# Inputs laid out in DRAM as they are read: weights by panel, cached keys by head dimension, values and states by head; new rows leave as they lie

## The chip, the cores and the metric

The kernel runs on one core of one Trainium2 chip. The metric is the device time of one execution in microseconds (us), the median of the runs. Arrays are laid out on the host before the launch, and what the host does with them is no part of the time. The engines are named as in the profile: PE (TensorE) with PEld for its weight loads, DVE (VectorE), ACT (ScalarE), POOL (GpSimd), SP (SyncE). DMAs are issued by SP, ACT and POOL, each on a queue of its own.

## The reference

One inference step of a layer with two groups of heads, for 1024 frames of one new stream (the prompt) and 16 frames of each of 8 running streams (the sample, 128 rows), in float32:

```
h = rms_norm(x) * norm_pre                      # x: 2048 wide
q_sb,k_sb,v_sb,gate_sb,q_r,k_r,v_r,gate_r = split(h @ w_in, 8)   # 8 x 1024, 8 heads of 128 each
A: z = q_sb k_sb^T / sqrt(128)                  # strictly causal; the sample also sees 1024 cached keys
   a = sigmoid(z) * cumprod_from_the_right(sigmoid(-z)),  o = a v_sb
B: rotary on q_r, k_r; retention in chunks of 64 with decay per head, state S (128 x 128);
   the sample starts from state_ret
y = concat(head_norm(o) * silu(gate)) @ w_out;  x + rms_norm(y) * norm_post
```

Returned are the new x of prompt and sample, the new keys and values of both, and the new states of both.

## The kernel before, in words

All weights, and the activations that meet them, are split into a high and a low part (float32r: `split`, L135, an ACT copy and a DVE subtraction), and each product is made of three matmuls. The rows are worked in two groups: group 0 holds the prompt tiles 0 to 3 and the sample, group 1 the tiles 4 to 7. For each group a loop runs over 8 heads (called 1 to 8 here), and each head makes its panels: `project` (L234, one column panel of 128 from `load_w`, 16 k-tiles of 128 rows in four loads of 256 KB) and, for two heads at once, `project_rows` (L293, values, eight loads of 256 KB). The loaded chunk is `wr` (or `wrn`), its parts `wh` and `wl`; four buffers each.

What the heads do beside their projections runs as jobs: Python generators that yield the number of ticks after which they go on. Each step of a projection calls `tick`, which lets one job make one step. This, with a scheduler that may put an instruction ahead of others that would wait, fixes the order of instructions on each engine; at run time each engine takes its own in that order. The numbers of ticks are the table `D_*`.

The jobs that matter here:

- `sb_branch` with `stick_breaking`, per head: scores `z` of a tile (L593), sigmoids `kp` and `be` on ACT (L505, L506), a select on POOL (L511), a scan and a product on DVE (L522, L523), then a turn of the weights through DRAM: `turn_out` writes `s_be`, `turn_in` reads it back in four loads (L486), a DVE transpose (L583) finishes it. The tile's output is `pa` (L623).
- `decode`, per head in group 0: the sample's scores against the cached keys, in two sets (`zc`, L672), and against its own keys (`zn`, L714); then the same weights, turned through `s_bd`; then the sum over the cached values in two sets of matmuls (`pd`, L741). Keys `kcT` and values `vc` share six buffers (tag `kv`).
- `ret_branch` and `retention`: `rk` is turned through `s_rk`, the decay table `dT` is loaded by SP, scores `rs` (L768) are multiplied by it (`sc`, L770), and `pa` (L786) follows.
- `keys_out`: transposes the new keys `kT` into rows (`kn`) and stores them 32 columns at a time.

A chunk of cached keys is loaded so:

```
for i in range(4):
    nc.gpsimd.dma_start(
        kc[32 * i : 32 * i + 32, :].rearrange("p (k d) -> p k d", d=32),
        cache_k[0, 2 * c + j, s * 512 : (s + 1) * 512, h, 32 * i : 32 * i + 32].rearrange("(k p) d -> p k d", p=32),
    )
...
turned = nc.vector.transpose(ready[-1][:, m % 2, :], loaded.pop(0))
```

DVE's transpose works in squares of 32 by 32, so the four loads place the squares and the transpose turns each. After the last head, `out_panel` and `out_project` multiply by `w_out` (L1066 to L1068), and the results are normed and stored.

Of the kernel before, what the change touches and what calls it, by code (L numbers as in the profile page):

```python
# [16 lines left out]
P = 128  # L17
D = 2048
# [13 lines left out]
D_REST = 8  # L32
KC_AHEAD = 2
D_DEC = 2
D_NAT = (8, 11)
# [3 lines left out]
D_AV = (9, 11)  # L39
D_ZC = 12  # L40
D_ROW = 18
D_KN = 40
D_VC = (6, 46)
# [22 lines left out]
def tile_hybrid_step(  # L66
# [7 lines left out]
    norm_pre,  # L74
    w_in,
    sb_gain,
# [188 lines left out]

    col = lambda i, h: i * H * P + h * P

    def project_rows(g, mov, col, dst, off, loads=None):
# [5 lines left out]
        for w in range(KT // 2):  # L274
            wr = wp.tile([P, 2, 2 * P], F32, name="wrn", tag="wr")
            nc.sync.dma_start(
                wr,
                w_in[0, 2 * w * P : 2 * (w + 1) * P, col : col + 2 * P].rearrange("(k p) e -> p k e", p=P),
            )
            for _ in range(WQ if loads and w == 0 else 0):  # L280
# [26 lines left out]
    with ExitStack() as s1:  # L307
# [152 lines left out]
        def store_rows(tiles, n, off, dst_p, dst_s, h):  # L460
            nc.scalar.dma_start(
                dst_p[0, 0, tiles[0] * P : (tiles[0] + 4) * P, h, :].rearrange("(t p) d -> p t d", p=P),
                n[:, off : off + 4, :],
            )
            if SAMPLE in tiles:
                nc.scalar.dma_start(
                    dst_s[0].rearrange("b t h d -> (b t) h d")[:, h, :], n[:, off + 4, :]
                )

# [166 lines left out]
        def decode(h, qs, rest):  # L636
# [9 lines left out]

            def chunk(m):
                s, r = divmod(m, NB)
                j, c = divmod(r, 4)
                return s, j, c  # L650

            def load(m):
                s, j, c = chunk(m)
                kc = ip.tile([P, 512], F32, name="kc", tag="kc", bufs=3)
                for i in range(4):
                    nc.gpsimd.dma_start(  # L656
                        kc[32 * i : 32 * i + 32, :].rearrange("p (k d) -> p k d", d=32),
                        cache_k[0, 2 * c + j, s * 512 : (s + 1) * 512, h, 32 * i : 32 * i + 32].rearrange(
                            "(k p) d -> p k d", p=32
                        ),  # L660
                    )
                return kc

            loaded, ready = [], []
            for m in range(-KC_AHEAD, 2 * NB + 1):
                if m > 0 and m % NB == 0:
                    s, _, _ = chunk(m - NB)
                    z = score_tile("zc")
                    for j in range(2):
                        for c in range(4):  # L670
# [3 lines left out]
                                qp[:, j, r],  # L674
                                ready[2 * j + c // 2][:, c % 2, :],
                                start=(j == 0),
                                stop=(j == 1),
                            )
                            if j == c == 0:

                                tc.add_manual_dep(
                                    mm.ins,
                                    turned.ins.name,
                                    mybir.DependencyInfo(
                                        mybir.DependencyClass.NoSync, mybir.DependencyReason.SCHED_ONLY
                                    ),
                                    reason="a set at a time",
                                )
                    ready = []
                    with tc.issue_after(mm.ins):  # L690
                        with_scores()
                    sigmoids(kp, be, s * 512, z)
                if 0 <= m < 2 * NB:
                    if m % 2 == 0:
                        ready.append(ip.tile([P, 2, 512], F32, name="kcT", tag="kv", bufs=V_BUFS))
                    turned = nc.vector.transpose(ready[-1][:, m % 2, :], loaded.pop(0))  # L696
                    yield D_ZC
                if m + KC_AHEAD < 2 * NB:
                    loaded.append(load(m + KC_AHEAD))
            def load_v(k):  # L700
                vc = ip.tile([P, NB, P], F32, name="vc", tag="kv", bufs=V_BUFS)
                ld = nc.sync.dma_start(
                    vc, cache_v[0, :, k * P : (k + 1) * P, h, :].rearrange("b p d -> p b d")
                )
                if 2 <= k < V_BUFS:
                    tied(ld)
                return vc
# [108 lines left out]
        def sample_retention(h, out, sc, rq, rkn, rv):  # L816
# [57 lines left out]
            for c in range(4):  # L874
                nc.scalar.dma_start(s_sample[0, 2 * c : 2 * c + 2, h].rearrange("b d e -> d b e"), sts[c])

# [20 lines left out]
        def sb_branch(gi, g, h, out, q2, k2, kT, rest):  # L897
            tiles, nt = g["tiles"], len(g["tiles"])
            off = 0 if gi == 0 else 4
            def keys_out():  # L900
                kn = ep.tile([P, nt * P], F32, name="kn", tag="rkn")
                nc.vector.transpose(kn, kT[:, : nt * P])
                for i in range(4):
                    q, ds = slice(32 * i, 32 * i + 32), slice(32 * i, 32 * i + 32)
                    nc.scalar.dma_start(
                        k_prompt[0, 0, tiles[0] * P : (tiles[0] + 4) * P, h, ds].rearrange("(j b) a -> b j a", b=32),
                        kn[q, : 4 * P].rearrange("p (j a) -> p j a", a=32),
                    )
                    if SAMPLE in tiles:
                        nc.scalar.dma_start(  # L910
                            k_sample[0].rearrange("b t h d -> (b t) h d")[:, h, ds].rearrange("(j b) a -> b j a", b=32),
                            kn[q, 4 * P :].rearrange("p (j a) -> p j a", a=32),
                        )
                yield 1

            Job(keys_out(), D_KN)
            if gi == 0:
# [279 lines left out]

_INS = [
    "x_prompt", "x_sample", "cache_sb_k", "cache_sb_v", "state_ret", "norm_pre", "w_in",
    "sb_head_norm", "ret_head_norm", "w_out", "norm_post",  # L1200
]
_OUTS = [
    (1, PT * P, D), (NB, DS, D), (1, 1, PT * P, H, P), (1, 1, PT * P, H, P), (1, 1, H, P, P),
    (1, NB, DS, H, P), (1, NB, DS, H, P), (1, NB, H, P, P),
]


# [60 lines left out]
```

## Time and profile before

| | |
|---|---|
| median of 3 runs | 2397.44 us (2394.52 to 2399.0) |
| profiled execution | 2393.5 us, its span 2391.8 us |
| mean granted TensorE clock | 0.991 |
| PE, DVE, ACT, POOL busy | 97%, 52%, 38%, 27% of the span |
| read from HBM, written | 336.24 MB, 79.69 MB |
| DMA packets | 677049, of them 224752 under 512 bytes |

How to read the page: its first part gives the busy time of each engine, its second the span in 40 slices (the digits are tenths), the groups give line, engine, operation, tiles out<-in, count, busy time and mean, and the idle time just before with what ended it. In a row of waits stand the waiting engine with its tile and line, what ended the wait, the sum in us, how often, and the longest. Group 0 runs from the start to about 1120 us, group 1 to about 1960 us, then the output projection.

### The profile page before, as it was taken

To read this page: it belongs to the slowest core of one execution; us is meant where nothing else is said; L and a number is where in the kernel's file an instruction comes from. 1 tells how busy PE (TensorE), PEld (TensorE's weight loads), DVE (VectorE), ACT (ScalarE), POOL (GpSimd) and SP (SyncE) were. 2 spreads that over 40 slices of the span, in tenths; PEclk is the share of its full clock that TensorE was granted. 3 is DMA by queue.
4 is the path that set the end of the run, shared out by engine and by line. 5 is a ranking of instruction groups with operands and counts; after the bars stand their busy time and mean duration, and the time that the engine had idled before them with its cause. 6 is when DMAs were issued, how large, how long until landed. Compare 5 with 4: busy or idle time off the path is not lost.

```text
span 2391.8 us, 40520 instructions
## 1 busy us (share of the span) xinstructions
PE 2320.5 (97%) x14832; PEld 2092.4 (87%) x14832; DVE 1255.6 (52%) x2442; ACT 920.0 (38%) x1937; POOL 644.1 (27%) x1033
## 2 busy tenths in 40 slices
PE   7999999999999999999899999999999999999998
PEld 7998899998999999998778989889898888888887
DVE  7245545455545555456545554554554566564544
ACT  6323333333333333334333334333343444443443
POOL 3144354434445353434202112020220220000000
PEclk9999999999999999999999999999999999999999
DMA  7659779796989979698866565555655666765563
GB/s 245 163 131 215 161 162 200 163 200 153 199 177 200 188 163 205 158 207 221 187 182 154 139 149 154 139 145 151 150 154 134 161 160 197 229 211 182 188 192 131
DMA packets 677049, 418.68 MB, mean 175 GB/s; under 512 B 224752, under 2 KB 620016, under 8 KB 674544
## 3 DMA queue, kind: packets, MB, share of 16 engines
q1 hardware_dynamic: 524272, 285.99, 48.0%
q0 software_dynamic: 32256, 71.36, 13.9%
q10 hardware_dynamic: 120320, 58.74, 9.1%
q8 instruction: 116, 1.90, 0.4%
q14 instruction: 85, 0.70, 0.1%
HBM read 336.24 MB, written 79.69 MB: 174 GB/s over the span
## 4 chain that ended last, share of the span: by engine, by line
PE 71%; DMA 6%; DVE 4%; issue 2%; ACT 2%; SPq 1%; POOL 0%; DVEq 0%; ACTq 0%; POOLq 0%
PE acc L234 36%; PE accn L293 12%; PE a L1067 5%; PE a L1066 5%; PE a L1068 5%; PE pa L623 2%; PE z L593 2%; DMA wr<-w_in 2%; PE zc L672 1%; PE pd L741 1%; DMA mr<-s_y 1%; DMA mr<-s_h 1%; DMA dT<-c_dt 1%; DVE wl L137 1%; PE pa L786 1%
## 5 line engine op out<-in xcount | busy, mean ns | idle before, releaser
L234 PE MATMUL acc<-mh,wh 128*128 128x256 f32 (+2 forms) x2304 | 667.2, 341 | 7.8 <-ACT wh L136 7.2
L137 DVE TENSOR_TENSOR wl<-wr,wh 128x512 fp32r<-128x512 f32 (+1 forms) x576 | 391.4, 684 | 517.7 <-ACT wh L136 500.8
L234 PE MATMUL acc<-ml,wh 128*128 128x256 f32 (+2 forms) x2304 | 661.5, 339 | 0.0
L234 PE MATMUL acc<-mh,wl 128*128 128x256 f32 (+2 forms) x2304 | 660.8, 339 | 0.0
L136 ACT ACTIVATE wh<-wr 128x512 fp32r<-128x512 f32 (+1 forms) x576 | 358.0, 625 | 726.6 <-PE acc L234 229.7
L234 PEld LDWEIGHTS acc<-mh,wh 128*128 128x128 f32 x2304 | 421.2, 189 | 40.5 <-ACT wh L136 9.0
L234 PEld LDWEIGHTS acc<-mh,wl 128*128 128x128 f32 x2304 | 424.5, 189 | 31.7 <-issue 2.5
L234 PEld LDWEIGHTS acc<-ml,wh 128*128 128x128 f32 x2304 | 425.5, 189 | 28.6 <-issue 0.8
L656 POOL DMA_DIRECT2D kc<-cache_sb_k x512 | 332.5, 655 | 344.4 <-DVE kcT L696 209.5
L293 PE MATMUL accn<-whn,mh 128*128 128x256 f32 x1152 | 329.2, 287 | 4.6 <-DVE rg L320 4.5
L293 PE MATMUL accn<-wln,mh 128*128 128x256 f32 x1152 | 326.3, 284 | 2.4 <-DVE wln L137 2.4
L293 PE MATMUL accn<-whn,ml 128*128 128x256 f32 x1152 | 325.9, 284 | 0.0
L293 PEld LDWEIGHTS accn<-whn,mh 128*128 128x128 f32 x1152 | 220.9, 192 | 8.5 <-DVE rg L320 4.8
L293 PEld LDWEIGHTS accn<-wln,mh 128*128 128x128 f32 x1152 | 221.7, 192 | 3.4 <-DVE wln L137 2.6
L293 PEld LDWEIGHTS accn<-whn,ml 128*128 128x128 f32 x1152 | 221.3, 192 | 0.0
L1067 PE MATMUL a<-wl,mh 128*128 128x512 f32 (+1 forms) x576 | 219.4, 381 | 1.1 <-DVE wl L137 1.1
L1066 PE MATMUL a<-wh,mh 128*128 128x512 f32 (+1 forms) x576 | 218.9, 381 | 0.1
L1068 PE MATMUL a<-wh,ml 128*128 128x512 f32 (+1 forms) x576 | 218.9, 380 | 0.0
L137 DVE TENSOR_TENSOR wln<-wrn,whn 128x512 fp32r<-128x512 f32 x128 | 87.3, 689 | 125.1 <-ACT whn L136 124.8
L136 ACT ACTIVATE whn<-wrn 128x512 fp32r<-128x512 f32 x128 | 79.6, 632 | 164.7 <-PE acc L234 70.7
L486 POOL DMA_DIRECT2D be<-s_be x128 | 94.3, 743 | 132.4 <-DMA s_be<-be 114.5
L1067 PEld LDWEIGHTS a<-wl,mh 128*128 128x128 f32 x576 | 108.3, 188 | 22.4 <-DVE wl L137 2.2
(195 smaller groups left out, 2617.6 us busy)
## 6 DMA issues: line engine op xcount, KB each, us to landing
wr<-w_in SPq DMA_DIRECT2D x384, 256.0 KB, 4.2
wr<-w_out SPq DMA_DIRECT2D x184, 256.0 KB, 3.6
wrn<-w_in SPq DMA_DIRECT2D x128, 256.0 KB, 3.3
kc<-cache_sb_k POOLq DMA_DIRECT2D x512, 64.0 KB, 4.7
vc<-cache_sb_v SPq DMA_DIRECT2D x64, 512.0 KB, 9.0
xt<-x_prompt SPq DMA_DIRECT2D x8, 1024.0 KB, 6.0
xr<-x_prompt SPq DMA_DIRECT2D x8, 1024.0 KB, 6.2
out<-out ACTq DMA_DIRECT2D x24, 256.0 KB, 3.4
```

The lines of the kernel that those rows point to most:

```text
L136: nc.scalar.activation(hi, src, AF.Copy)
L137: nc.vector.tensor_tensor(lo, src, hi.bitcast(F32), ALU.subtract)
L234: last = nc.tensor.matmul(a[:, :m], lhs[:, j, :], rhs[w][:, j, o : o + m], start=(w == 0 and j == 0 and n == 0), stop=(w == KT // WQ - 1 a ...
L293: anchor[0] = nc.tensor.matmul(a, lhs[q][:, jj, ts], rhs[:, j, :], start=(w == 0 and j == 0 and n == 0 and t % 2 == 0), stop=(w == KT // 2 ...
L486: q.dma_start(raw[32 * i : 32 * i + 32, :].rearrange("p (k a) -> p k a", a=32), s[:, :, 32 * i : 32 * i + 32].rearrange("k (j b) a -> b (k ...
L593: nc.tensor.matmul(z[:, :c], q2[a][:, i * P : (i + 1) * P], k2[b][:, s : s + c], start=(m == 0), stop=(m == 2),)
L623: nc.tensor.matmul(po[:, :P], at[:, j, :], vn[:, j, :], start=(j == 0), stop=(j == t))
L656: nc.gpsimd.dma_start(kc[32 * i : 32 * i + 32, :].rearrange("p (k d) -> p k d", d=32), cache_k[0, 2 * c + j, s * 512 : (s + 1) * 512, h, 3 ...
L672: mm = nc.tensor.matmul(z[r, :], qp[:, j, r], ready[2 * j + c // 2][:, c % 2, :], start=(j == 0), stop=(j == 1),)
L1066: nc.tensor.matmul(a[:, :width], hi[q][:, j, ts], wh, start=(k == 0), stop=False)
L1067: nc.tensor.matmul(a[:, :width], hi[q][:, j, ts], wl, start=False, stop=False)
L1068: nc.tensor.matmul(a[:, :width], lo[q][:, j, ts], wh, start=False, stop=(k == KT - 1))
```

## The change

The arrays get other layouts in DRAM, and the loads and stores follow them:

- `w_in` becomes two arrays: `w_cols` for the six column panels of each head, so that the 2 KB which a partition reads in one load lie together (before, four pieces of 512 bytes), and `w_rows` for the value panels (before, two pieces of 1 KB).
- `cache_k` has the head dimension on the partitions. A load of 512 KB brings two chunks as they are needed, 4 KB in one piece for each partition, right into the buffer of `kcT`. The tile `kc`, its 512 loads and the 128 transposes are gone. `decode` has 8 steps of 24 ticks for this where it had 16 of 12.
- `cache_v` and `state_ret` are laid out by head: a value load has 4 KB in one piece for each partition (before 8 pieces of 512 bytes), a state load 1 KB (before two of 512 bytes).
- New keys leave as `kT` lies, head dimension first, from ACT right after `kT` is made; the job `keys_out` with its transpose is gone. New values and states leave by head. The host puts them in the asked order.

```diff
+COLS = (0, 1, 3, 4, 5, 7)
+ROWS = (2, 6)
-D_ZC = 12
+D_ZC = 24
-D_KN = 40
...
@@ load_w, project_rows
-            nc.sync.dma_start(
-                wr,
-                w_in[0, w * WQ * P : (w + 1) * WQ * P, col : col + P].rearrange("(k p) e -> p k e", p=P),
-            )
+            nc.sync.dma_start(wr, w_cols[COLS.index(col[0]), col[1], :, w * WQ : (w + 1) * WQ, :])
...
-                w_in[0, 2 * w * P : 2 * (w + 1) * P, col : col + 2 * P].rearrange("(k p) e -> p k e", p=P),
+            nc.sync.dma_start(wr, w_rows[ROWS.index(col[0]), col[1] // 2, :, 2 * w : 2 * (w + 1), :])
...
@@ store_rows
-                dst_p[0, 0, tiles[0] * P : (tiles[0] + 4) * P, h, :].rearrange("(t p) d -> p t d", p=P),
-                n[:, off : off + 4, :],
+            nc.scalar.dma_start(dst_p[h, :, tiles[0] : tiles[0] + 4, :], n[:, off : off + 4, :])
...
@@ decode
-            loaded, ready = [], []
-            for m in range(-KC_AHEAD, 2 * NB + 1):
-                if m > 0 and m % NB == 0:
-                    s, _, _ = chunk(m - NB)
+            def load_k(m):
+                kc = ip.tile([P, 2, 512], F32, name="kcT", tag="kv", bufs=V_BUFS)
+                ready.append((kc, nc.gpsimd.dma_start(kc, cache_k[h, m // 4, m % 4])))
+
+            ready = []
+            for m in range(KC_AHEAD):
+                load_k(m)
+            for m in range(NB + 1):
+                if m > 0 and m % 4 == 0:
+                    s, ks = m // 4 - 1, ready[:4]
+                    del ready[:4]
...
-                                ready[2 * j + c // 2][:, c % 2, :],
+                                ks[2 * j + c // 2][0][:, c % 2, :],
...
-                if 0 <= m < 2 * NB:
-                    if m % 2 == 0:
-                        ready.append(ip.tile([P, 2, 512], F32, name="kcT", tag="kv", bufs=V_BUFS))
-                    turned = nc.vector.transpose(ready[-1][:, m % 2, :], loaded.pop(0))
+                if m + KC_AHEAD < NB:
+                    load_k(m + KC_AHEAD)
+                if m < NB:
                     yield D_ZC
-                if m + KC_AHEAD < 2 * NB:
-                    loaded.append(load(m + KC_AHEAD))
...
-                    vc, cache_v[0, :, k * P : (k + 1) * P, h, :].rearrange("b p d -> p b d")
+                ld = nc.sync.dma_start(vc, cache_v[h, k])
...
@@ sample_retention
-                tied(nc.sync.dma_start(st, state_ret[0, 2 * c : 2 * c + 2, h].rearrange("b d e -> d b e")))
+                tied(nc.sync.dma_start(st, state_ret[h, :, 2 * c : 2 * c + 2, :]))
...
@@ sb_branch
-            def keys_out():
-                kn = ep.tile([P, nt * P], F32, name="kn", tag="rkn")
-                nc.vector.transpose(kn, kT[:, : nt * P])
-                for i in range(4):
...
-            Job(keys_out(), D_KN)
+            nc.scalar.dma_start(k_prompt[h, :, tiles[0] * P : (tiles[0] + 4) * P], kT[:, :NB_TOK])
+            if SAMPLE in tiles:
+                nc.scalar.dma_start(k_sample[h], kT[:, 4 * P : 5 * P])
```

The numbers of lines are other ones after the change: the key loads L656 become L640, the selects L511 become L502, the turns L479 and L486 become L470 and L477, the weight loads L220 become L222, the value loads L702 become L680. The program has as many matmuls as before.

The order of instructions moves at two places that the prediction speaks of. The first is POOL's in the first head of group 0, before the change, from the store of the third tile's weights (`s_be_2`) to the read-back of the fourth's:

```order
L479 DMA s_be_2_2348<-kb 128x3x128
L511 AFFINE_SELECT kb<-kb 128x128 x2
L656 DMA kc<-cache_sb_k 32x16x32 x2
L486 DMA kb<-s_be_2_2348 32x12x32 x2
L511 AFFINE_SELECT kp<-kp 128x128
L511 AFFINE_SELECT be<-be 128x128
L517 AFFINE_SELECT kp<-kp 128x128
L517 AFFINE_SELECT be<-be 128x128
L486 DMA kb<-s_be_2_2348 32x12x32 x2
L479 DMA s_be_3_2513<-kb 128x4x128
L656 DMA kc<-cache_sb_k 32x16x32 x2
L486 DMA kb<-s_be_3_2513 32x16x32 x4
```

The same place on POOL after the change, with the key loads that follow for the second head:

```order
L470 DMA s_be_2_2255<-kb 128x3x128
L477 DMA kb<-s_be_1_2121 32x8x32 x4
L502 AFFINE_SELECT kb<-kb 128x128 x2
L470 DMA s_be_3_2440<-kb 128x4x128
L502 AFFINE_SELECT kp<-kp 128x128
L502 AFFINE_SELECT be<-be 128x128
L508 AFFINE_SELECT kp<-kp 128x128
L508 AFFINE_SELECT be<-be 128x128
L477 DMA kb<-s_be_2_2255 32x12x32 x4
L477 DMA kb<-s_be_3_2440 32x16x32 x4
L640 DMA kcT<-cache_k 128x1024 x6
```

The selects of `kp` and `be` are the sample's and need the sigmoids of `zn`. Before, they stood between the second and the third of the four read-backs of `s_be_2`; now all eight read-backs stand behind them. Between the read-backs and the next head stood single key loads; now six whole ones stand together.

The second place is SP's queue in the first head and the start of the second, before the change, from the first value loads (`vc`) to the decay table (`dT`) of the second head:

```order
L702 DMA vc<-cache_sb_v 128x8x128 x2
L220 DMA wr<-w_in 128x4x128 x4
L702 DMA vc<-cache_sb_v 128x8x128 x3
L220 DMA wr<-w_in 128x4x128 x2
L702 DMA vc<-cache_sb_v 128x8x128
L220 DMA wr<-w_in 128x4x128
L486 DMA be<-s_bd_2487 32x36x32 x4
L486 DMA ro<-s_rk_1_2720 32x20x32 x2
L702 DMA vc<-cache_sb_v 128x8x128 x2
L486 DMA ro<-s_rk_1_2720 32x20x32 x2
L486 DMA so<-s_o_0_4_0_2800 32x16x32 x4
L763 DMA dT<-c_dt 128x256
```

The same queue after the change (the first two value loads stand further ahead):

```order
L680 DMA vc<-cache_v 128x1024
L222 DMA wr<-w_cols 128x512 x3
L680 DMA vc<-cache_v 128x1024
L222 DMA wr<-w_cols 128x512
L477 DMA be<-s_bd_2391 32x36x32 x4
L680 DMA vc<-cache_v 128x1024 x2
L222 DMA wr<-w_cols 128x512 x2
L680 DMA vc<-cache_v 128x1024 x2
L222 DMA wr<-w_cols 128x512 x2
L477 DMA ro<-s_rk_1_2624 32x20x32 x4
L477 DMA so<-s_o_0_4_0_2706 32x16x32 x4
L739 DMA dT<-c_dt 128x256
```

The last two value loads stood in the middle of the read-backs of `rk`; now they stand four weight loads ahead of them. On PE the two sets of value matmuls of this head stood 20 projection matmuls apart and now stand 74 apart, and `zn` stands some 90 projection matmuls earlier.

More of the change, by code (lines that the diff above doesn't have):

```diff
@@ L74, in tile_hybrid_step @@
     norm_pre,
-    w_in,
+    w_cols,
+    w_rows,
     sb_gain,
@@ L1256 @@
     data = {n: np.ascontiguousarray(inputs[n]) for n in _INS}
+    data.update(_laid_out({n: np.asarray(a) for n, a in inputs.items()}))
     data.update(_constants())
@@ L1266 @@
     r = run_bass_kernel_spmd(nc, [data], core_ids=[0])
-    return tuple(r.results[0][f"out_{i}"] for i in range(len(_OUTS)))
+    got = [np.asarray(r.results[0][f"out_{i}"]) for i in range(len(_OUTS))]
+    return tuple(np.ascontiguousarray(a) for a in _as_asked(*got))
```

81 lines of the change are left out of this document (35 added, 46 removed).

## The prediction

> **What bounds the kernel now.** The page comes first: its busy times, then the rows by slice.
>
> ```profile
> span 2391.8 us, 40520 instructions
> PE 2320.5 (97%) x14832; PEld 2092.4 (87%) x14832; DVE 1255.6 (52%) x2442; ACT 920.0 (38%) x1937; POOL 644.1 (27%) x1033
> DMA  7659779796989979698866565555655666765563
> ```
>
> TensorE is busy for 97% of the span; VectorE, which loses work here, for 52%. The change leaves every matmul as it is, so what can be won is the time in which TensorE waits, and the time in which its clock is lowered after a wait. The DMA engines are close to full in the slices 5 to 20 (group 0) and have room later. Next I read the waits of TensorE alone: the sum of the waits in us, their number, the longest.
>
> ```profile
> PE p0t L379 <- DVE dg L396: 10.7, 1, 10.7
> PE pa L786 <- DVE sc L770: 8.2, 6, 3.9
> PE acc L234 <- ACT wh L136: 7.2, 3, 5.2
> PE pa L623 <- DVE kb L583: 6.4, 2, 4.8
> PE pa L623 <- DVE kp L583: 5.0, 6, 1.1
> PE accn L293 <- DVE rg L320: 4.5, 1, 4.5
> PE pd L741 <- DMA vc<-cache_sb_v: 4.2, 2, 2.3
> PE accn L293 <- DVE wln L137: 2.4, 1, 2.4
> PE zc L672 <- DVE kcT L696: 1.7, 2, 1.5
> ```
>
> These make 50.3 us. The first row is the start (x and its norm) and the fifth lies in group 1; the change touches neither. The others lie in group 0, where the cache is read. Then the stretches around the long ones, in the table by window (length, busy times, then PEclk, the share of the DMA engines, GB/s):
>
> ```profile
> 230.00:237.00 7.00, 5.64 (x31) 5.64 (x32) 2.14 (x5) 1.76 (x5) 4.52 (x7) 0.76 1.06 271
> 258.00:270.00 12.00, 7.83 (x58) 5.97 (x51) 3.34 (x13) 1.89 (x4) 5.16 (x9) 0.72 0.95 159
> 540.00:550.00 10.00, 6.15 (x33) 5.88 (x33) 8.27 (x23) 3.41 (x9) 5.18 (x9) 0.83 1.13 222
> 1110.00:1125.00 15.00, 10.46 (x66) 6.81 (x65) 8.96 (x16) 7.41 (x16) 7.47 (x12) 0.77 0.85 235
> 1140.00:1150.00 10.00, 7.98 (x54) 7.98 (x55) 7.92 (x17) 3.75 (x7) 6.99 (x12) 0.83 0.72 129
> 1208.00:1220.00 12.00, 6.85 (x36) 3.84 (x34) 3.66 (x10) 3.47 (x8) 0.00 (x0) 0.72 0.88 236
> ```
>
> In each of the six stretches a wait of 2.4 us or more is followed by a lower clock. Length times (1 - PEclk) is what that costs: 1.7, 3.4, 1.7, 3.4, 1.7 and 3.4 us, together 15.3. A wait is thus dearer than its length.
>
> **The change part by part.** *Keys of the cache.* 512 loads of 64 KB in pieces of 128 bytes, and 128 transposes, become 64 loads of 512 KB that land turned.
>
> ```profile
> L656 POOL DMA_DIRECT2D kc<-cache_sb_k x512 | 332.5, 655 | 344.4 <-DVE kcT L696 209.5
> L696 DVE STREAM_TRANSPOSE kcT<-kc 128x512 f32<-128x512 f32 x128 | 88.4, 699 | 33.8 <-DMA kc<-cache_sb_k 31.0 <-PE pd L741 2.2 <-issue 0.4
> ```
>
> GpSimd loses 448 issues of 655 ns (293 us), VectorE 88.4 us and the 31.0 us in which its queue stood behind a key load. Neither bounds the kernel, so the sum books none of it, only the waits of TensorE that hang on it. The 2.4 us wait for `wln` at 1142 us is one. The chain shows what VectorE stood behind just before:
>
> ```profile
> 1134.89 4.86 DMA kc<-cache_sb_k
> 1139.77 0.71 DVE kcT L696
> ```
>
> It goes with its clock: 2.4 + 1.7 = 4.1 us (0 if the split before it is late for another reason). The 1.7 us on `kcT` become a wait for a load and are not booked.
>
> *Read-back of the first head.* GpSimd's part of the timeline:
>
> ```profile
> 207.13 1.23 POOL L486 DMA_DIRECT2D kb<-s_be  x2 [3.77 <-DMA s_be<-kb]
> 220.30 0.29 POOL L511 TENSOR_SCALAR_AFFINE_SELECT kp<-kp 128x128 f32<-128x128 f32 x1 [11.94 <-ACT kp L505]
> 221.38 1.23 POOL L486 DMA_DIRECT2D kb<-s_be  x2
> ```
>
> Two of four loads of the third tile's weights were queued behind a select that waited 11.9 us for the sample's last scores (`zn`), and TensorE then waited 4.8 us. All four now stand behind that select, but `zn` moves ahead by some 90 projection matmuls, and the select with it. What a projection matmul takes, start to start, the chain gives:
>
> ```profile
> 360.50 11.74 PE acc L234 x80
> ```
>
> That is 0.147 us each, so the select comes 13 us earlier. All of it goes: 4.8 + 1.7 = 6.5 us. With no cover left the same 4.8 us would stay.
>
> *Values of the cache.* 64 loads of 512 KB, from pieces of 512 bytes to 4 KB. In the first head the order puts 74 products between the two sets of value matmuls where 20 stood, so that the last two loads, which need buffers of the first set, have 11 us instead of 3 (at 0.147 us). How fast a landing gets is bounded by rows of the same size and unlike pieces (issues, KB, us to landing):
>
> ```profile
> wr<-w_in SPq DMA_DIRECT2D x384, 256.0 KB, 4.2
> wr<-w_out SPq DMA_DIRECT2D x184, 256.0 KB, 3.6
> vc<-cache_sb_v SPq DMA_DIRECT2D x64, 512.0 KB, 9.0
> xt<-x_prompt SPq DMA_DIRECT2D x8, 1024.0 KB, 6.0
> ```
>
> `w_in` comes in pieces of 512 bytes, `w_out` of 2 KB: 4.2 against 3.6 us. A value load takes 9.0 us, an x load of twice the size, in rows of 8 KB, 6.0. So landings get shorter by between 0 and a third; I take the seventh that the weights show. With 11 us of room the wait goes in either case: 4.2 + 3.4 = 7.6 us. The Trainium skill, "DMA: Bandwidth & Descriptors", Specifications, puts the smallest transfer for full rate at 512 bytes; by that the weights and values would win nothing. The rows of 4.2 and 3.6 us lean the other way, in different stages of the program.
>
> *Weights.* 512 loads of 256 KB, same number and buffers. They are mostly hidden; one was not, at 1203 us on SyncE's queue and on the chain:
>
> ```profile
> 1202.37 1.02 SPq L702 DMA_DIRECT2D vc<-cache_sb_v  x2
> 1203.44 9.48 DMA wr<-w_in
> ```
>
> It stood behind two value loads that waited for their buffers, and TensorE waited 5.2 us for `wh`. The order there is unchanged; shorter pieces of the queue in front take about half: (5.2 + 3.4) / 2 = 4.3 us, with 0 and 8.6 as ends. The gate's wait at 1116 us (`rg`) had ScalarE behind loads of `mr`, which are left alone but share the DMA engines (ScalarE's timeline):
>
> ```profile
> 1113.39 1.22 ACT L136 ACTIVATE mh<-mr 128x512 fp32r<-128x512 f32 x2 [3.15 <-DMA mr<-s_h]
> ```
>
> The same half: (4.5 + 3.4) / 2 = 4.0, between 0 and 7.9.
>
> *Decay table.* In the heads 2 to 8 the first scores need `dT`, which SyncE issues after the read-backs (SyncE's timeline, the chain, GpSimd's timeline):
>
> ```profile
> 534.01 4.60 SPq L486 DMA_DIRECT2D so<-s_o  x4
> 538.66 1.31 SPq L763 DMA_DIRECT2D dT<-c_dt  x1
> 538.66 5.75 DMA dT<-c_dt
> 526.00 4.52 POOL L656 DMA_DIRECT2D kc<-cache_sb_k  x7 [24.13 <-DVE kcT L696]
> ```
>
> That gave the 3.9 us wait; the five others of the row share 4.3. I take the long one down to the 0.9 of the rest, which also spares its clock (3.0 + 1.7), and half of the 4.3 (2.1): 6.8 us. Ends: 9.9 won, or a loss (second rival).
>
> *Stores and states.* New keys leave from `kT` at once: 16 transposes and 96 short stores become 24 stores, issued by ScalarE, which waited 17.5 us for those.
>
> ```profile
> L902 DVE STREAM_TRANSPOSE kn<-kT 128x640 f32<-128x640 f32 (+1 forms) x16 | 12.4, 773 | 9.2 <-ACT kT L992 9.2
> ACT kb L506 <- DMA out<-kn: 17.5, 6, 3.8
> ```
>
> ScalarE is busy for 38%; booked at nothing. If that cover failed it would be 17.5 us. The stores of values and states keep their number.
>
> **The sum.** 4.1 + 6.5 + 7.6 + 4.3 + 4.0 + 6.8 = 33.3 us. Against it stand new waits, since places move by some us in every head of group 0: the fourth tile's scores come 16 to 19 us of products later in heads 2 to 7. The nearest row is group 1, 5.0 us in 6 waits; I book 1 us in each of seven heads. Net 26.3. The profiled execution took 2393.5 us (span 2391.8), so 2367.2; the median of the three runs, 2397.4, lies 3.9 above it: **2371 us**.
>
> The Trainium skill, "TensorE: Matmul & The Clock Gate", Part 1, has the array go to half clock after an idle window of about 3.4 us. Here a wait of 2.4 us was enough (1140 to 1150: 0.83), so the trace disagrees on the length. By that rule the halved waits at 1116 and 1213 us would shed all their clock and the sum would win 3.4 us more.
>
> **The rivals.**
>
> 1. *Long rows bring nothing.* Landings stay as they are and only the order helps: 6.5 + 7.6 + 4.1 - 7 = 11.2 us won, 2382.3 + 3.9 = 2386. For it: most landings are hidden, and at 1.13 the DMA share beside `dT` says that bytes were waiting, not pieces. Against: 4.2 and 3.6 us.
>
> 2. *The keys come in a burst, and `dT` lands behind it: slower.* GpSimd's key loads were paced by VectorE's transposes (209.5 us of waiting in the row of L656). Now they wait for buffers alone, and four of the six that open a head wait for the last value matmuls of the head before, 3 to 6 us ahead of `dT`. They bring 2 MB. By the rows of 1024 KB in 6.0 us and 256 KB in 3.6 a KB more takes 3.1 ns: 6.4 us in whole, 3.2 for half. If half of it lies in front of `dT`, seven heads lose 3.2 + 1.7 of clock = 34.3 us; the rest of the sum without `dT` wins 26.5 - 7 = 19.5; the net is 14.8 slower, 2412 us (in whole, 2435). It decides from 19.5 / 7 = 2.8 us a head, or 1.1 us of lateness where that trips the clock. For it: four heads are late by about 1 us now. Against: SyncE's own queue clears faster, and in the head at 526 us seven old key loads went out in just that place. The Trainium skill, "DMA: Bandwidth & Descriptors", Queues, rings and completion order, has each engine take turns between queues packet by packet; by that rule `dT` would not stand behind the whole burst. No row here separates the two.
>
> 3. *Nearly all comes back.* 4.8 + 4.2 + 8.2 + 4.5 + 2.4 + 7.2 + 1.7 = 33.0, and 15.3 of clock, with no new waits: 2345.2 + 3.9 = 2349.
>
> 4. *The waits only change their names*, since each stream's places were set for the old work: 2397.
>
> **How the numbers follow.** Forecast 0.52, first rival 0.20, second 0.11, third 0.12, fourth 0.05. A measurement here tells 0.2% (4.8 us) from no change, so faster is below 2392.6. Faster: 0.52 + 0.12 + 0.17 of the first rival's 0.20 = 0.81. Slower: the second and 0.01 of the fourth = 0.12. The rest, 0.07, is the same. The range 2350 to 2396 holds the forecast, the first rival and most of the third; left out are the second, a third of the third and half of the fourth, 0.18.
>
> **What would show it.** Right: TensorE busy within 20 us of 2300, waits of TensorE near 30 us, PEclk 1.00 from 230 to 270; no row of TensorE on `kb` above 2 us or on `vc`; `wr` landing near 3.6 us. The first rival shows as landings of 4.2 us with `wh` and `sc` waits as before; the second as a row of `sc` above 20 us with `dT` landing later than 6 us. The forecast is wrong if the waits of TensorE stay near 50 us, or if its busy time moves by more than the clock explains.

## The result and the profile after

The kernel after takes 2355.31 us (median of 4 runs, 2351.69 to 2357.42), the kernel before beside it 2395.98 (4 runs): a ratio of 0.9831, 95% interval 0.9809 to 0.9852. The change makes the kernel faster by 1.7%; 2371 us was forecast, in a range of 2350 to 2396. The profiled execution took 2351.69 us.

The page of the kernel after, the rows that answer to those of before:

```profile
span 2349.9 us, 39636 instructions
PE 2307.7 (98%) x14832; PEld 2088.4 (89%) x14832; DVE 1174.4 (50%) x2298; ACT 923.6 (39%) x1937; POOL 353.3 (15%) x585
DMA  7546657575666656577665555555555576775653
```

The span is 41.9 us shorter. TensorE's busy time fell by 12.8 us with the same matmuls, so the other 29.1 us are time in which it stood still. The waits of TensorE in the kernel after (sum in us, number, longest):

```profile
PE p0t L375 <- DVE dg L392: 10.7, 1, 10.7
PE pa L614 <- DVE kp L574: 4.5, 5, 1.1
PE pa L614 <- DVE ro L771: 3.2, 1, 3.2
PE pSs L842 <- ACT be L497: 3.1, 1, 3.1
PE accn L289 <- DVE rg L316: 0.7, 1, 0.7
```

The first two are the start and group 1, as before. The third and the fourth are new, the gate's wait is down from 4.5 us to 0.7, and the rows on `sc`, `wh`, `kb`, `vc`, `wln` and `kcT` that stood in the table of before are gone or below 1 us. The table by window, first the six stretches of before, then the two new waits (length, busy times, PEclk, share of the DMA engines, GB/s):

```profile
230.00:237.00 7.00, 7.00 (x51) 7.00 (x50) 4.00 (x10) 3.17 (x8) 0.00 (x0) 1.00 0.18 64
258.00:270.00 12.00, 12.00 (x88) 12.00 (x86) 7.18 (x19) 4.22 (x12) 0.00 (x0) 1.00 0.84 287
540.00:550.00 10.00, 10.00 (x73) 10.00 (x73) 4.16 (x10) 5.17 (x12) 0.00 (x0) 1.00 0.48 149
1110.00:1125.00 15.00, 15.00 (x111) 14.22 (x110) 5.97 (x11) 6.91 (x12) 5.35 (x8) 1.00 0.55 139
1140.00:1150.00 10.00, 10.00 (x49) 8.27 (x48) 5.90 (x17) 5.41 (x11) 0.00 (x0) 1.00 0.97 248
1208.00:1220.00 12.00, 12.00 (x81) 11.04 (x80) 5.17 (x6) 5.03 (x10) 3.33 (x6) 1.00 0.50 139
1096.00:1102.00 6.00, 4.84 (x32) 4.53 (x33) 5.75 (x13) 5.04 (x12) 3.73 (x6) 0.72 0.81 266
1930.00:1936.00 6.00, 5.06 (x24) 4.67 (x25) 4.30 (x11) 2.73 (x9) 2.36 (x3) 0.72 0.58 151
```

The full clock holds in the six stretches, where other work now stands, up to 44 us further on. It holds elsewhere too: between the start and the end of the program the two last rows are the only places with a lower one (PEclk is 1.00 from 25 to 1096 us, from 1102 to 1930 and from 1936 to 2340). Length times (1 - PEclk) is 1.7 us in each of these two: the lowered clock costs 3.4 us instead of 15.3, and the difference, 11.9 us, is nearly the whole fall of the busy time. The DMA issues of the kernel after (KB each, median us to landing):

```profile
wr<-w_cols SPq DMA_DIRECT2D x384, 256.0 KB, 3.8
kcT<-cache_k POOLq DMA_DIRECT2D x64, 512.0 KB, 8.1
vc<-cache_v SPq DMA_DIRECT2D x64, 512.0 KB, 5.9
dT<-c_dt SPq DMA_DIRECT2D x16, 128.0 KB, 3.5
```

Value loads land in 5.9 us instead of 9.0. So the waits went as the prediction's third rival had it, nearly all of them. Which part of the change did that, and whether by the reasons given, the two profiles can't say: the order moved, and four layouts and the stores changed at once.

### The profile page after: what moved, and what is told of

It reads as the page before. It is cut to its first block, busy times and chain, and to the rows that moved or that the text cites. A ratio compares the mean times of both kernels' runs of the same rounds, so it can differ in the third digit from the quotient of the medians.

```text
span 2349.9 us, 39636 instructions
## 1 busy us (share of the span) xinstructions
PE 2307.7 (98%) x14832; PEld 2088.4 (89%) x14832; DVE 1174.4 (50%) x2298; ACT 923.6 (39%) x1937; POOL 353.3 (15%) x585
## 3 DMA queue, kind: packets, MB, share of 16 engines
q0 software_dynamic: 25088, 71.33, 10.2%
## 4 chain that ended last, share of the span: by engine, by line
PE 89%; DMA 4%; DVE 3%; ACT 2%; issue 1%; SPq 0%; DVEq 0%; ACTq 0%
PE acc L233 48%; PE accn L289 16%; PE a L1029 4%; PE a L1030 4%; PE a L1028 4%; PE pa L614 3%; PE z L584 2%; DMA mr<-s_y 2%; PE pd L717 1%; PE zc L653 1%; DMA mr<-s_h 1%; PE pa L762 1%; PE rs L744 1%; PE pS L777 1%; DVE ml L139 1%
## 5 line engine op out<-in xcount | busy, mean ns | idle before, releaser
L1028 PEld LDWEIGHTS a<-wh,mh 128*128 128x128 f32 x576 | 108.3, 188 | 21.5 <-ACT wh L138 0.8
L1030 PEld LDWEIGHTS a<-wh,ml 128*128 128x128 f32 x576 | 108.3, 188 | 20.4
```

The lines of the kernel that those rows point to most:

```text
L1028: nc.tensor.matmul(a[:, :width], hi[q][:, j, ts], wh, start=(k == 0), stop=False)
L1030: nc.tensor.matmul(a[:, :width], lo[q][:, j, ts], wh, start=False, stop=(k == KT - 1))
```

## Experiments

**One part at a time.** Four kernels, each the kernel before with one part of the change; they ran on one chip (before: 2388.14 us there).

Weights alone (`w_only`); the order on every engine is that of before.

```diff
-nc.sync.dma_start(wr, w_in[0, w * WQ * P : (w + 1) * WQ * P, col : col + P].rearrange("(k p) e -> p k e", p=P))
+nc.sync.dma_start(wr, w_cols[COLS.index(col[0]), col[1], :, w * WQ : (w + 1) * WQ, :])
```

> Only the weights are laid out by panel; the order of the instructions on TensorE stays as before, so this is a test of landing times alone. My theory (longer pieces land sooner): the wr landing falls from 4.2 to about 3.8 us, the half of the wait for wh at 1213 us, of the gate's at 1116 us and part of the dT waits go: 8 to 11 us faster, about 2386. Rival (long rows bring nothing): 2396, wr landing 4.2 us, the same waits of TensorE as before.

Measured: 2383.73 us, ratio 0.999 (0.9976 to 1.0004). Its DMA row and four of its waits:

```profile
wr<-w_cols SPq DMA_DIRECT2D x384, 256.0 KB, 4.2
```

```profile
PE acc L234 <- ACT wh L139: 6.3, 3, 5.5
PE pa L620 <- DVE kb L580: 5.5, 2, 4.2
PE pd L738 <- DMA vc<-cache_v: 4.0, 2, 3.2
PE pa L783 <- DVE sc L767: 2.5, 4, 1.2
```

Pieces of 2 KB land no sooner than those of 512 bytes did (4.2 us both times), and the first three waits stay. The row on `sc` is shorter than before (2.5 us instead of 8.2); what shortened it was not followed up. In the time the weights' layout alone brings nothing that can be told from noise: by the interval it is 0.24% at most.

Cached keys alone (`k_only`). This moves the order as the whole change does: `zn` earlier, 74 products between the sets of value matmuls.

```diff
-for i in range(4): nc.gpsimd.dma_start(kc[32 * i : 32 * i + 32, :]...)      # 512 loads of 64 KB
-turned = nc.vector.transpose(ready[-1][:, m % 2, :], loaded.pop(0))
+ready.append((kc, nc.gpsimd.dma_start(kc, cache_k[h, m // 4, m % 4])))     # 64 loads of 512 KB
```

> Only the cached keys change (layout, 64 loads instead of 512, no transposes); this moves the order as the whole change does, with 74 projection matmuls between the two value sets of the first head. My theory: the kb wait at 231 us (6.5 with its clock), the vc waits at 261 us (7.6) and the wln wait at 1142 us (4.1) go: 11 to 18 us faster, 2378 to 2385, PEclk 1.00 from 230 to 270. Burst rival: the dT waits grow in the heads 2 to 8, sc above 20 us, no gain or slower. If this alone gives 25 us or more, the weights and values are worth little.

Measured: 2401.5 us, ratio 1.0062 (1.0047 to 1.0077): slower. The wait that this brings and what is left of the gate's (`rg`), the burst on GpSimd's timeline, what stands on SyncE's at the same time, and the table by window after the first and after the third of the new waits:

```profile
PE pa L773 <- DVE sc L757: 29.5, 8, 5.2
PE accn L293 <- DVE rg L320: 0.5, 1, 0.5
```

```profile
393.57 2.20 POOL L649 DMA_DIRECT2D kcT<-cache_k  x4 [11.09 <-PE pd L728]
```

```profile
393.93 5.41 SPq L486 DMA_DIRECT2D so<-s_o  x4
399.38 1.90 SPq L750 DMA_DIRECT2D dT<-c_dt  x1
```

```profile
267.00:275.00 8.00, 5.67 (x32) 5.67 (x33) 6.16 (x20) 2.88 (x8) 0.00 (x0) 0.79 0.81 233
541.00:550.00 9.00, 6.53 (x31) 6.53 (x32) 6.05 (x19) 3.03 (x9) 0.00 (x0) 0.62 0.75 215
```

Four loads of 512 KB go out on the release of the value buffers, the decay table lands 7.5 to 9.2 us after the first `rs` of its head, the products up to the first `pa` leave room for some 5.7 us (39 at 0.147), and seven heads wait. Four of these waits cost 1.7 us of clock besides, like the first (8.00 x 0.21), and three cost 3.4, like the third (9.00 x 0.38): 17.1 us together.

In its place and its size this is the prediction's second rival, but not in its path. That one had the table's own transfer take longer behind the burst. Here the table takes 2.3 to 5.9 us from issue to landing, no longer than before (3.9 to 5.8); it is issued later. In the heads 3 to 8 SyncE takes 14.5 us from the first read-back of `ro` to the table where it took 10.8 before (means of six), and its waits for other engines are only 0.3 us of that (1.4 before): while the burst is out, the issuing itself is slower.

The waits on `kb`, `vc` and `wln` are gone here too, with the values laid out as before, and that on the gate falls from 4.5 us to 0.5.

Values and states alone (`vs_only`); the order on every engine is that of before.

```diff
-ld = nc.sync.dma_start(vc, cache_v[0, :, k * P : (k + 1) * P, h, :].rearrange("b p d -> p b d"))
+ld = nc.sync.dma_start(vc, cache_v[h, k])
-tied(nc.sync.dma_start(st, state_ret[0, 2 * c : 2 * c + 2, h].rearrange("b d e -> d b e")))
+tied(nc.sync.dma_start(st, state_ret[h, :, 2 * c : 2 * c + 2, :]))
```

> Only cached values and states are laid out by head; the order stays as before, with 3 us between the two value sets of the first head. My theory: the value landing falls from 9.0 to about 6 us, so of the vc waits of 4.2 us some 2 remain and the clock after them (3.4) may stay or go, and about half of the wh wait at 1213 us goes: 5 to 9 us faster, about 2389. Rival (long rows bring nothing): 2396.

Measured: 2355.27 us, ratio 0.9868 (0.9853 to 0.9883): nearly all of it. Its value loads and its waits:

```profile
vc<-cache_v SPq DMA_DIRECT2D x64, 512.0 KB, 5.7
```

```profile
PE accn L293 <- DVE rg L320: 4.5, 1, 4.5
PE pa L784 <- DVE sc L768: 1.8, 2, 1.1
PE pa L623 <- DVE kb L583: 1.1, 1, 1.1
```

The wait on `kb` shrinks from 6.4 to 1.1 us, the one on `sc` from 8.2 to 1.8, and the one on `vc` goes, with `zn` and the 20 products where they were. The order wasn't needed for any of them. The gate's wait stays at 4.5 us.

For `kb` this shows what the prediction's reading left out. The select still waits for the sample's last scores, as long as before:

```profile
220.44 0.29 POOL L511 TENSOR_SCALAR_AFFINE_SELECT kp<-kp 128x128 f32<-128x128 f32 x1 [11.55 <-ACT kp L505]
```

The two read-backs still go out behind it, at 221.5 us. But they land 5.0 and 5.2 us later, where before it was 8.7 and 8.9. Three value loads, issued at 217.6 us before and 217.8 here, are on their way at the same time; the last of them lands at 230.0 us before and at 225.1 here.

Stores alone (`o_only`).

```diff
-Job(keys_out(), D_KN)
+nc.scalar.dma_start(k_prompt[h, :, tiles[0] * P : (tiles[0] + 4) * P], kT[:, :NB_TOK])
```

> Only the outputs change: new keys leave as kT lies, values and states by head; the job with the transposes of the new keys is gone. The prediction booked this at nothing: 2396, within 5 us. Rival: the 17.5 us that ScalarE waited for those stores, and SyncE's waits for them, were on the path: up to 17 us faster, about 2380.

Measured: 2389.58 us, ratio 1.0008 (0.9995 to 1.002). Nothing, as booked.

**Why the values?** They differ from before in two things: a load of 512 KB has 128 pieces of 4 KB instead of 1024 of 512 bytes, and it comes from one stretch of DRAM. Three kernels take these apart, and one leaves the keys as they were (before on that chip: 2389.01 us; `v_pad` and `v_far`, below, ran on another, 2387.24).

Values without the states (`v_only`): the first two lines of the diff above.

> Cached values alone by head; the states, the weights, the keys and the stores as in the kernel before. Theory A (the value loads' 1024 short pieces hold up SyncE's queue and all that is queued behind them): ratio 0.985 to 0.989, as with the values and states together (0.987), value loads landing in 5.7 us, no wait of TensorE on sc, kb, vc or wln above 2 us. Rival B (the states' loads and stores, 64 of each, carry a good part of it): ratio 0.992 or more, with some of the sc and kb waits still there.

Measured: 2352.97 us, ratio 0.9853 (0.9839 to 0.9867). It is the values.

```profile
DMA to landing us min/median/max: 3.6/5.5/10.7
```

Values by head, but in the old pieces (`v_short`); here as in the next two the order on every engine is that of before.

```diff
+"cache_v": a(inputs["cache_sb_v"][0].reshape(NB, 8, P, H, P).transpose(3, 1, 0, 2, 4))
+ld = nc.sync.dma_start(vc, cache_v[h, k].rearrange("b p d -> p b d"))
```

> Cached values alone by head, so that each load of 512 KB comes from one contiguous stretch, but still in 1024 pieces of 512 bytes; all else as before. Theory A (the number and length of the pieces): nothing is won, ratio 0.998 to 1.002, value loads landing in 8.5 to 9 us. Rival C (what costs is that the pieces lie 64 KB apart across the whole cache, not that they are short): landings of 6 us and a ratio of 0.985 to 0.99. In between (7 us, 0.993) it is some of both.

Measured: 2361.98 us, ratio 0.9885 (0.9872 to 0.9897). The landing of `vc` in before, and here:

```profile
DMA to landing us min/median/max: 5.9/9.0/12.9
```

```profile
DMA to landing us min/median/max: 4.2/6.3/13.3
```

This is a kernel with as many pieces of the same length in the same order; only the addresses in DRAM differ. (The rows of one load lie 4,096 bytes apart in the kernel before, not the 64 KB that the expectation gives.) It has over three quarters of the gain (1.15% of 1.47%), and Theory A, with the prediction's reading of the landings, falls. The longer pieces add the rest: 2352.97 against 2361.98 us, intervals apart.

An empty ninth head behind each row (`v_pad`): the kernel's own value load as before, the rows 4,608 bytes apart.

```diff
-"cache_v": a(inputs["cache_sb_v"]),
+"cache_v": np.pad(inputs["cache_sb_v"], ((0, 0), (0, 0), (0, 0), (0, 1), (0, 0))),
```

> Cached values as they lie in the kernel before, in 512-byte pieces, but with an empty ninth head behind each row, so that the pieces of one load are 4,608 bytes apart instead of 4,096 (and the eight sequences 4,718,592 bytes instead of 4,194,304); the order on every engine is that of the kernel before. Theory F (pieces a power of two apart get into each other's way): healed as by the contiguous stretch, ratio 0.985 to 0.990, value loads landing in 6 to 6.5 us. Rival G (pieces that are not neighbours cost, at whatever distance): ratio 0.998 to 1.002, landing in 8.5 to 9 us.

Measured: 2361.83 us, ratio 0.9891 (0.9876 to 0.9906). Padding alone wins as much as the contiguous stretch:

```profile
DMA to landing us min/median/max: 4.1/6.7/12.5
```

Heads ahead of rows, the blocks of the eight sequences 4 MB apart (`v_far`).

```diff
+"cache_v": a(inputs["cache_sb_v"][0].transpose(0, 2, 1, 3)),
+ld = nc.sync.dma_start(vc, cache_v[:, h, k * P : (k + 1) * P, :].rearrange("b p d -> p b d"))
```

> Cached values by sequence, head and row, in 512-byte pieces: the 128 pieces of one sequence are neighbours (a block of 64 KB), the eight blocks of a load lie 4 MB apart as before; the order on every engine is that of the kernel before. Theories F and G both: the neighbours heal it, ratio 0.985 to 0.990, landing in 6 to 6.5 us. Rival H (the 4 MB between the blocks are what costs, not the 4 KB between the rows): ratio 0.998 to 1.002, landing in 8.5 to 9 us; half and half would be 0.994 and 7.5 us.

Measured: 2361.02 us, ratio 0.9889 (0.9873 to 0.9905).

```profile
DMA to landing us min/median/max: 4.4/6.7/13.3
```

So it isn't that the pieces are no neighbours (`v_pad`: they are not, and it heals), nor that the eight blocks lie 4 MB apart (`v_far`: they do, and it heals). What the slow layout has and the three quick ones lack is rows exactly 4,096 bytes apart. `v_pad` moves the sequences off 4 MB as well, so whether 4 KB between rows would do harm without 4 MB between sequences was not tried.

How that reaches TensorE in the wait on the decay table is read from SyncE's timeline in one head (the same instructions in the same order), first before, then `v_pad`:

```profile
511.62 1.63 SPq L702 DMA_DIRECT2D vc<-cache_sb_v  x2
513.34 5.61 SPq L220 DMA_DIRECT2D wr<-w_in  x2
519.04 3.93 SPq L702 DMA_DIRECT2D vc<-cache_sb_v  x2
527.70 6.20 SPq L486 DMA_DIRECT2D ro<-s_rk  x4
```

```profile
497.23 1.46 SPq L702 DMA_DIRECT2D vc<-cache_v  x2
498.79 2.46 SPq L220 DMA_DIRECT2D wr<-w_in  x2
506.42 1.81 SPq L702 DMA_DIRECT2D vc<-cache_v  x2
510.13 5.82 SPq L486 DMA_DIRECT2D ro<-s_rk  x4
```

The rows of the four value loads and the two weight loads between them make 11.2 us before (1.63 + 5.61 + 3.93) and 5.7 us in `v_pad`. That isn't issuing alone: 4.3 us of the 5.61 are a wait that VectorE ends. The two weight loads land 10.2 and 12.2 us after their issue before, and 6.1 and 5.4 us after it in `v_pad`. Behind these loads stand the read-backs of `ro` and `so` and the decay table. The first scores of the head, which VectorE multiplies by this table, start on TensorE at

```profile
534.98 0.38 PE L768 MATMUL rs<-rq,rk 128*128 128x128 f32 x2
```

```profile
522.97 0.38 PE L768 MATMUL rs<-rq,rk 128*128 128x128 f32 x2
```

that is 7.3 us behind the first read-back of `ro` before, and 12.8 us in `v_pad`: SyncE's lead over TensorE grew by 5.6 us. Of these, 2.4 us were there already at the first value load shown (25.7 us ahead of the scores instead of 23.4), and 3.2 us were won over these lines, although in `v_pad` SyncE stands 5.2 us ahead of the second pair of value loads, until the value matmuls release a buffer. Before, the table lands 9.4 us after these scores (538.66 + 5.75) and TensorE, with room for 5.7 us, waits; in `v_pad` it lands 4.1 us after them, and there is no wait.

The whole change without the keys (`no_k`): weights, values, states and stores as after, keys as before.

> The whole change but the cached keys: 512 key loads of 64 KB in pieces of 128 bytes and 128 transposes remain. If the keys harm as they do alone (1.006): ratio 0.977 to 0.980, faster than the whole change (0.983). If their burst is harmless once SyncE's queue clears sooner, and their transposes were in VectorE's way: ratio 0.985 to 0.988, slower than the whole change.

Measured: 2354.54 us, ratio 0.9854 (0.984 to 0.9869), as the values alone (0.9853). The kernel after itself, timed again beside `v_pad` and `v_far` (`after_again`):

> The kernel after, timed beside the three others: ratio 0.981 to 0.985 (0.983 on its first chip). Against the values alone and the change without the keys (both 0.985 on one chip) it tells whether the keys bring anything once the values are by head: if they do, 0.983 or less.

Measured: 2354.09 us, ratio 0.9854 (0.9836 to 0.9873). The keys, the weights and the stores together bring nothing beside the values that these runs can tell; a difference of 0.2% either way would not show, and the kernels to compare ran on two chips, each beside its own before. The harm that the keys do alone is gone as well: in the kernel after the table lands at most 4.3 us after the first `rs`, where the keys alone had 7.5 to 9.2.

**Why do the keys alone cost?** In `k_only` the table is late by its issue, behind the read-backs. It could be issued ahead of them, unless its bytes then wait. `k_dt` is `k_only` with the table's load moved ahead of the four read-backs of `so`:

```diff
 turn_in(s, raw, nc.sync)
+dT = op.tile([P, 2, P], F32, name="dT", tag="dT", bufs=1)
+tied(nc.sync.dma_start(dT, c_dt[:, h]))          # was at the start of retention()
 yield D_TI[phase[0]]
```

> Cached keys alone (ratio 1.006 with its 29.5 us of waits on sc), with one load moved: the decay table is issued on SyncE right after the read-backs of ro, ahead of the four of so, instead of behind them. Theory D (the table is late because SyncE's queue stands 5 to 6 us behind those read-backs while the burst goes on; it lands 4 to 6 us after its issue anyway): the sc waits fall from 29.5 us to under 5, their seven lowered clocks go, ratio 0.988 to 0.993. Rival E (prediction's second rival in its own words: the table's bytes wait behind the burst's bytes on the DMA engines): its landing goes from 5 to 8 us or more and more than half of the sc waits stay, ratio 1.000 to 1.006.

Measured: 2400.92 us (12 runs, 2381.72 to 2410.89), ratio 1.0043 (1.0024 to 1.0062). The row of `sc`, and the table on the chain of waits:

```profile
PE pa L770 <- DVE sc L754: 29.5, 8, 6.4
```

```profile
392.77 8.79 DMA dT<-c_dt
530.33 8.99 DMA dT<-c_dt
```

Over the seven heads the table was issued 5.8 us earlier against the first `rs` than in `k_only` (1.7 us ahead of it instead of 4.1 behind, in the mean) and landed only 2.0 us earlier (6.7 us after it instead of 8.7): from issue to landing it took 6.6 to 9.5 us instead of 2.3 to 5.9. So Theory D falls in its premise, and the figures that Rival E gave came; while the burst is out, most of what an earlier place in the queue wins is lost in the transfer. The sum of the waits can't be used as expected, because the order on TensorE moved too: in `k_dt` the first `pa` stands 20 instructions behind `rs` instead of 39, which takes away 2.8 us of room (19 at 0.147). Four read-backs of `ro` were still ahead of the table, so whether its bytes waited behind theirs or behind the keys' is open as well.

**One more buffer.** The old key tiles left 6 KB per partition free. `after_v7` gives values and keys a seventh buffer of 4 KB.

```diff
-V_BUFS = 6
+V_BUFS = 7
```

> The kernel after with seven buffers for values and keys instead of six (the 6 KB per partition of the old key tiles are free). The last value load but one no longer waits for the first set's buffers and one of the opening key loads goes out earlier. If the waits that are left (31 us, 15 of them at the start) hang on those buffers, as the one on be at 1097 us may: ratio 0.979 to 0.982. If they don't: 0.983, as after. A longer queue in front of the read-backs would show as a row of kb or sc and 0.985 or more.

Measured: 2346.56 us (2344.93 to 2351.46), ratio 0.983 (0.9813 to 0.9847), beside 2354.09 us (2348.87 to 2357.69) for the kernel after on the same chip. It is 1.7% faster than the kernel before. Against the kernel after its median is 7.5 us lower, but the two intervals overlap by 0.0011, so that is likely and not settled. (The 0.983 that the expectation gives for no effect is the kernel after's ratio in its first runs; beside this kernel it had 0.9854.) Its waits:

```profile
PE accn L289 <- DVE rg L316: 3.1, 1, 3.1
PE pa L614 <- DVE ro L771: 2.6, 1, 2.6
PE pSs L842 <- ACT be L497: 2.0, 1, 2.0
```

The wait on `be` is shorter, one on `rg` is back. With 10.7 us at the start and 4.5 in group 1 that no layout here touches, there is little left to win in this way.

## Why the prediction was right, and where it was not

- *What bounds the kernel, and what a wait costs:* right. 29.1 us of waits and 12.8 us of busy time went; the clock's share was put at 15.3 us before and is 3.4 after. One reading was off: at 261 us there is no wait of 2.4 us, but two of 1.9 and 2.3. The third rival (2349 us) was nearest in its working: of its 33.0 us of waits almost all went, and two new ones came back.
- *Values, 7.6 us:* the wait itself went, and the order is enough for it: `k_only` has no row on `vc` with value loads of 8.5 us. What failed is the reading of the landings. They were to get shorter by a seventh, read from `w_in` against `w_out` as an effect of the pieces' length; they got shorter by a third, and mostly not through their length. And the term covered only the waits on `vc`. What quicker value loads give to the read-backs, the table and the weights was booked under other names: alone they bring 36 us (`v_only`). (On SyncE's queue the last two value loads now stand two weight loads ahead of the read-backs of `rk`, not four.)
- *Read-back of the first head, 6.5 us:* it went, but not only by the order. The order with the old values takes the whole row (`k_only`), and the values with the old order bring it from 6.4 to 1.1 us (`vs_only`), with the select as late as ever. The late select was one part of the cause, the slow landing of the two loads behind it another.
- *Decay table, 6.8 us:* the waits on `sc` went nearly whole and with them the clock; with the values alone 1.8 us (`vs_only`) or 0.8 us (`v_only`) are left.
- *Weights, 4.3 us, and gate, 4.0 us:* "shorter pieces of the queue in front" was to halve them. The weights' pieces do nothing that shows in the time (0.999); nearly the whole of `wh` and all but 0.7 us of `rg` went in the kernel after. `wh` goes mostly with the values (2.8 us left in `vs_only`, 0.9 in `v_only`), `rg` with the keys (0.5 us in `k_only`, 4.5 in `vs_only`). These two terms and the table's were booked at 15.1 us, with 26.4 as their best ends (8.6 + 7.9 + 9.9); that they came out near those ends is most of what the forecast lacked. The forecast of 3.6 us for the landing of `wr` came nearly true (3.8), for another reason: the keys alone bring it to 3.7 without touching the weights.
- *Keys, 4.1 us:* wrong in sign for the keys by themselves. The wait on `wln` goes, but seven heads wait for the table. The second rival had 3.2 us a head and 34.3 us in all; `k_only` shows 29.5 us and 17.1 of clock, 46.6 us. Of its two signs the row of `sc` came and a table landing later than 6 us did not (2.3 to 5.9): the table was late by its issue. The harm shows only with the old values. Its chance of 0.11 was for the whole change, where the condition that was named against it ("SyncE's own queue clears faster") held.
- *New waits, 7 us:* 6.3 us and 3.4 of clock came, not in seven heads but in one at the end of group 0 (`be`) and one in group 1 (`ro`). The first comes with the keys (4.0 us in `k_only`, 0.5 in `no_k`), the second with the stores (2.4 us in `o_only`, 2.2 in `no_k`, 0.8 at most in the kernels with the old stores).
- *Stores at nothing:* right in the time (1.0008), though they bring the wait on `ro`.
- *The first rival* (the order helps, the rows don't) is refuted: the values alone win 1.5% with the old order (`v_only`), and with the new order and the old values the kernel is slower (`k_only`). For the length of the rows by itself its name is not far off, as the next point says.
- *The rule of 512 bytes.* By the Trainium skill, "DMA: Bandwidth & Descriptors", Specifications, weights and values would win nothing from longer pieces. The prediction leaned against it; for length alone the rule was close to what the runs show: nothing for the weights, 0.4% for the values.

That the sum came within 16 us is in part luck. It named the waits rightly and gave each a cause of its own. The runs show two causes, and they overlap: the quicker value loads take most of the waits on `sc`, `wh`, `kb` and `vc`, and the keys' layout with its order takes `kb`, `vc`, `wln` and `rg`. Since each wait was counted once, the reasons could be wrong and the sum still hold. The signs that were named for being right came too (TensorE busy for 2307.7 us, no row on `kb` or `vc`, `wr` landing in 3.8 us), and they don't tell these causes apart.

## What to carry to other kernels

A list of waits isn't a list of causes: where several of them stand behind one queue, or have their loads out at the same time, look for the load that lands slowly for its size, and cost the relief for all of them. Before rearranging an array whose rows lie a power of two apart, pad them by one piece: here that showed the trouble without touching the program's order, and won three quarters of what the values' new layout wins (1.1% of 1.5%). Fewer, larger loads that wait for buffers alone come in bursts; a small load that is needed soon should be landed ahead of them, since 5.8 us of lead in its queue brought 2.0 here.

## What the runs showed of the hardware

- Value loads of 512 KB in 1024 pieces of 512 bytes landed in 9.0 us (median of 64) with rows 4,096 bytes apart and in 6.7 us with rows 4,608 bytes apart. The packet records of SyncE's queue in the 64 stretches from issue to landing hold, each packet counted once, 1,130 of 512 bytes that took over 150 ns before, and 137, 183 and 158 in `v_short`, `v_pad` and `v_far`; the mean hardly moves (36.2 ns against 35.2, 35.0 and 35.0). What can be seen of it is a few slow packets, not a slowness of all. What makes them slow no run shows.
- The Trainium skill, "DMA: Bandwidth & Descriptors", Latency and other measured facts, has a row on row pitches at large powers of two, with rates that fall from a pitch of 512 KiB to one of 4 MiB and come back with a pad of 4 KiB, not with one of 192 bytes. The runs agree in kind; here rows 4 KB apart, in eight sequences 4 MB apart, were enough, and a pad of 512 bytes in each row healed them. It isn't every power of two: the pieces of `w_in` lie 32 KB apart, and laying them together left the landing at 4.2 us.
- A load of 128 KB took 6.6 to 9.5 us in the seven heads of `k_dt`, in which it went out together with four loads of 512 KB on another queue, and 2.3 to 5.9 us in `k_only`, where it went out 5.8 us later against the first scores.
- SyncE's issuing got slower while such a burst was out: nine loads in a row took 14.5 us from the first to the last issue in `k_only` and 10.8 us before (means of six heads), with 0.3 and 1.4 us of waits in them.
- The clock was lowered for 3.4 us or for twice that after waits of TensorE of 2.3 to 5.2 us (the seven of `k_only`: 1.7 us lost four times, 3.4 us three times). The loss doesn't follow the length of the wait: 3.8 us cost 3.4 at 818 us and 1.7 at 682 us.
